# Hybrid encoder step on one core: the order of instructions made with the scheduler's timeline model

## The chip, the cores and the metric

The kernel runs on one core of a Trainium2 chip. TensorE (PE) multiplies matrices and writes its results to PSUM; VectorE (DVE), ScalarE (ACT) and GpSimd (POOL) work on tiles and run beside it; SyncE (SP) mostly issues the transfers. Each engine takes its own instructions in a fixed order, and waits on semaphores for what other engines make. The metric is the device time of one execution in microseconds (us), the median of several.

## The reference

One layer of a streaming encoder for 512 prompt frames and 8 x 16 frames of running streams (640 tokens), model width 2048:

```python
h = rmsnorm(x, p['norm_mix_g'][l])
proj = h @ p['w_in'][l]
...
o_gdn, gdn_conv_new, gdn_S_new = gdn_mixer(...)
...
x = x + jnp.concatenate([o_gdn, o_fox, o_lru], axis=-1) @ p['w_out'][l]
f_out, ffn_conv_new = conv_ffn(rmsnorm(x, p['norm_ffn_g'][l]), ...)
x = x + f_out
```

Three mixers share the input projection: GDN (4 heads, a gated delta rule: per 64-frame chunk a triangular system is solved, then a matrix state is carried on), FoX (8 heads, attention with a forget gate, with a cache of 512 rows for the running streams) and LRU (4 blocks of a gated linear recurrence). The feed-forward part multiplies by `w_up` (two times 5632 columns), convolves and gates, and multiplies by `w_down`. A last norm follows. All of it is fp32.

## The kernel before

Tokens lie along the free dimension, in two halves of 320 columns (`HALF`). Each large matmul is made of three fp32r products, high x high, high x low and low x high: a weight tile is split on ACT into its high part (L134 `whi`, or L1102 `wh` in the feed-forward part) and on DVE into the rest (L135 `wlo`, L1107 `wl`). These 128 x 128 by 320 matmuls (L146 with PSUM tiles `d`, L1143 with PSUM tiles `p`) I call dense.

**Input projection and mixers (to about 860 us).** The heads are projected in the order G0 L0 F0 G1 L1 F1 F2 G2 L2 F3 F4 G3 L3 F5 F6 F7. The mixers are generators that `drive` moves on by one step after each dense piece of work, so that in the source dense matmuls stand between the steps of a mixer. A GDN head solves its triangular system by levels (L628 to L653, a loop over `l` from 1 to 6): PE multiplies M by Z (L633), DVE masks the product (L638), PE multiplies by X (L643), DVE subtracts it from Z (L645), PE transposes Z (L651), ACT copies it back to X (L653). Each step needs the one before. Ahead of the loop stand q and k products (L596), transposes (L517) and copies (L599, L603, L607). The last level takes L618, L621 (ACT), L626 and L628. The PSUM tiles of these steps are `mm` (one buffer) and `m` (three); `d` has three.

**Output projection and norm (to 1223 us).** Two halves, with the first weights of the feed-forward part prepared beside them.

**Up (1223 to 2282 us).** For each of 44 column blocks f, a Winograd-Strassen scheme makes seven products of 8 weight tiles each (`wino`, L1143): seven of the eight PSUM banks are taken by `pf1` in the order of `SEQP`, so that each bank of the next block is one that the block before it used one product earlier. `combine` (L1154 to L1160, with L1435 and L1436 as its gate) reads the seven products and so frees the banks. The weights come by SP; DVE forms three sums of each tile (L1088 to L1090), and L1102 and L1107 split it. `wh` and `wl` have three buffers each, the raw tile `w` five. The gated result goes to HBM (`hT`).

**Down (2282 to 2850 us).** The rows of hT come back as 22 hops of two tiles `f` (L1467, two buffers), whose sums (L1061 to L1063) and split (ACT L1071, DVE L1073) `form` makes, up to 8 hops ahead of the matmuls. 32 visits of `down` make products as above, combine them (L1492 and L1493 in the place of the gate) and add them to HBM. `ending` does the last norm.

**What sets the order.** The source is one program; the tile framework takes all its instructions and orders them on each engine by a model of their times, keeping what depends on what. `drive` and the place in the source only give the priorities. The model is chosen where the context is opened, in the last lines of the program (L1844).

## Time and profile before

| what | us |
|---|---|
| median of 3 runs | 2877.57 (2876.38 to 2877.73) |
| profiled execution | 2873.5 |
| its span, first to last instruction | 2871.7 |
| PE busy | 2827.9 |
| DVE busy | 2141.7 |
| ACT busy | 1034.3 |
| mean granted clock of TensorE | 0.993 |

The profiled execution is 4.1 us below the median. In rows of the profile a line such as L633 is a line of the kernel, followed by the operation, the tile that is written and those that are read, and in square brackets the time that the engine sat idle before it and whose result ended that. Windows give the busy time of each engine between two times, then the granted clock (1.00 is full speed).

### The profile page before, as it was taken

How to read it: one execution, taken by the hardware profiler on the slowest of the kernel's cores; microseconds unless marked ns; L12 is line 12 of the kernel's file. 1: busy time of each engine (PE TensorE's matmuls, PEld its weight loads, DVE VectorE, ACT ScalarE, POOL GpSimd, SP SyncE). 2: the span in 40 equal slices, each digit the busy share in tenths (PEclk: the TensorE clock that was granted, in tenths of full speed). 3: DMA queues.
4: the chain of work that ended last, by engine and by line, in shares of the span. 5: the costliest groups of instructions: out<-in, count | busy, mean ns of one | idle time of the engine just before them, and what ended most of it. 6: DMA issues, size and time to landing. Idle time of an engine off the chain costs nothing. (4 is left out here: it accounts for less than half of the span.)

```text
span 2871.7 us, 51107 instructions
## 1 busy us (share of the span) xinstructions
PE 2827.9 (98%) x19823; PEld 2754.8 (96%) x19823; DVE 2141.7 (75%) x4723; ACT 1034.3 (36%) x1439; POOL 280.5 (10%) x481
## 2 busy tenths in 40 slices
PE   9899999999999999999999999999999999999997
PEld 8899999999999999999999999999999999999997
DVE  5746545644644536898888888988888999898877
ACT  5233323323322413443333333333333444344333
POOL 1000000000000001011101111111111010000003
PEclk9899999999999999999999999999999999999998
DMA  8123143134124646433333333333333365555545
GB/s 302 41 100 113 62 151 124 61 129 140 59 101 166 237 154 197 157 106 102 99 99 97 100 99 104 107 98 100 101 99 99 119 165 160 142 149 150 125 118 140
DMA packets 169060, 356.81 MB, mean 124 GB/s; under 512 B 19432, under 2 KB 24504, under 8 KB 168816
## 3 DMA queue, kind: packets, MB, share of 16 engines
q1 hardware_dynamic: 153104, 306.63, 33.2%
q0 software_dynamic: 15712, 46.91, 7.4%
q8 instruction: 155, 2.54, 0.4%
q14 instruction: 89, 0.73, 0.1%
HBM read 294.07 MB, written 59.39 MB: 123 GB/s over the span
## 5 line engine op out<-in xcount | busy, mean ns | idle before, releaser
L1143 PE MATMUL p<-x,wh 128*128 128x320 f32 x7280 | 1604.8, 309 | 7.2 <-DVE u L1155 2.8
L1143 PEld LDWEIGHTS p<-x,wh 128*128 128x128 f32 x7280 | 1215.9, 188 | 14.9 <-DVE u L1155 4.9
L1143 PE MATMUL p<-x,wl 128*128 128x320 f32 x3640 | 1121.5, 309 | 0.5 <-DVE wl L1107 0.5
L1102 ACT CAST wh<-w 128x896 fp32r<-128x896 f32 x520 | 490.6, 943 | 964.8 <-PE p L1143 705.8
L1143 PEld LDWEIGHTS p<-x,wl 128*128 128x128 f32 x3640 | 682.8, 188 | 0.8 <-DVE wl L1107 0.8
L1107 DVE TENSOR_TENSOR wl<-w,wh 128x896 fp32r<-128x896 f32 x520 | 564.6, 1086 | 116.4 <-ACT wh L1102 74.4
L146 PE MATMUL d<-xh,whi 128*128 128x320 f32 x1488 | 387.8, 326 | 3.1 <-DVE t L218 2.6
L146 PE MATMUL d<-xl,whi 128*128 128x320 f32 x1488 | 365.1, 310 | 0.2 <-DVE xl L184 0.2
L146 PE MATMUL d<-xh,wlo 128*128 128x320 f32 x1488 | 363.0, 310 | 0.2 <-DVE wlo L135 0.2
L134 ACT CAST whi<-raw 128x512 fp32r<-128x512 f32 x226 | 139.4, 619 | 450.1 <-PE d L146 407.4
L135 DVE TENSOR_TENSOR wlo<-raw,whi 128x512 fp32r<-128x512 f32 x226 | 155.1, 688 | 158.3 <-ACT whi L134 157.1
L146 PEld LDWEIGHTS d<-xh,whi 128*128 128x128 f32 x1488 | 250.3, 189 | 12.7 <-DVE t L218 4.1
L146 PEld LDWEIGHTS d<-xl,whi 128*128 128x128 f32 x1488 | 255.6, 188 | 0.8 <-DVE xl L184 0.5
L146 PEld LDWEIGHTS d<-xh,wlo 128*128 128x128 f32 x1488 | 254.6, 188 | 0.7 <-DVE wlo L135 0.4
L1088 DVE TENSOR_TENSOR w<-w 128x256 f32<-128x256 f32 x520 | 216.1, 417 | 51.9 <-DMA w<-in_w_down 48.6
L1090 DVE TENSOR_TENSOR w<-w 128x128 f32<-128x128 f32 x520 | 148.1, 285 | 6.2
L1089 DVE TENSOR_TENSOR w<-w 128x128 f32<-128x128 f32 x520 | 146.7, 284 | 4.1
L257 DVE SCALAR_TENSOR_TENSOR t<-t,prm,t 128x656 f32<-128x656 f32 (+1 forms) x136 | 122.3, 899 | 5.1 <-ACT t L253 4.4
L1429 POOL COPY t<-ns_fc 128x16 f32<-128x16 f32 x44 | 95.6, 2173 | 0.2 <-issue 0.2
L1499 POOL DMA_DIRECT2D x<-t x48 | 42.0, 1018 | 382.9 <-DVE t L1493 358.2
L1073 DVE TENSOR_TENSOR x<-f,x 128x960 fp32r<-128x960 f32 (+1 forms) x58 | 76.2, 1315 | 0.2 <-ACT x L1071 0.2
L1071 ACT CAST x<-f 128x960 fp32r<-128x960 f32 (+1 forms) x58 | 64.1, 1126 | 30.5 <-DVE f L1063 13.5
(420 smaller groups left out, 2851.8 us busy)
## 6 DMA issues: line engine op xcount, KB each, us to landing
w<-in_w_up SPq DMA_DIRECT2D x352, 256.0 KB, 2.6
raw<-in_w_in SPq DMA_DIRECT2D x192, 256.0 KB, 2.7
w<-in_w_down SPq DMA_DIRECT2D x176, 256.0 KB, 2.8
x<-t POOLq DMA_DIRECT2D x80, 320.0 KB, 4.4
kc<-in_ckT SPq DMA_DIRECT2D x32, 512.0 KB, 5.0
vc<-in_cv SPq DMA_DIRECT2D x32, 512.0 KB, 5.6
hT<-t POOLq DMA_DIRECT2D x44, 320.0 KB, 2.5
f<-hT SPq DMA_DIRECT2D x44, 320.0 KB, 3.4
```

The source lines that it names most:

```text
L134: nc.scalar.copy(hi[:, :n], raw[:, :n])
L135: nc.vector.tensor_sub(lo[:, :n], raw[:, :n], hi[:, :n].bitcast(F32))
L146: self.nc.tensor.matmul(ps[h][:, :HALF], wt[:, w], x[:, h * HALF:(h + 1) * HALF], start=start and i == 0, stop=stop and i == 2)
L257: nc.vector.scalar_tensor_tensor(out[:, :n], x[:, j:j + n], w[:, j:j + 1], out[:, :n], op0=OP.mult, op1=OP.add)
L1073: nc.vector.tensor_sub(l3[:, a:b], f[:, a:b], h3[:, a:b].bitcast(F32))
L1088: nc.vector.tensor_tensor(w[:, 4:6], w[:, 0:1].to_broadcast([P, 2, P]), w[:, 2:4], op=OP.add)
L1089: nc.vector.tensor_add(w[:, 6], w[:, 4], w[:, 3])
L1090: nc.vector.tensor_add(w[:, 7], w[:, 1], w[:, 6])
L1102: nc.scalar.copy(hi[:, 0:n], part)
L1107: self.nc.vector.tensor_sub(lo[:, 0:n], part, hi[:, 0:n].bitcast(F32))
L1143: nc.tensor.matmul(ps[p], l[:, wi], r[:, xi], start=i == 0 and j == 0, stop=i == n - 1 and j == 2)
L1429: nc.gpsimd.tensor_copy(so[:, :, :2], ns_fc[:, f, 1:, :])
```

## The change

The scheduler is asked for its other model, which keeps a timeline of the engines; nothing else in the source differs.

```diff
-    with tile.TileContext(nc) as tc:
+    with tile.TileContext(nc, schedule_with_timeline_sim=True) as tc:
         body(tc, a, cfg)
```

The two programs have the same instructions on each engine; their order differs on all of them. Three places follow. Names carry running numbers; `mm`, `m`, `d`, `p` are PSUM tiles, `t` and `u` temporaries.

**PE, first level of the solve of GDN head G1.** Before (from L517, the transposes into mm_448, to the M x Z product, and the first dense matmuls after it):

```order
L517 MATMUL mm_448_2979<-cst0_86,t_441_2936 128x128 x5
L146 MATMUL d_453_3026<-xl0_125,whi_439_2921 128x320
L146 MATMUL d_453_3026<-xh0_123,wlo_440_2922 128x320
L146 MATMUL d_453_3026<-xh0_123,whi_439_2921 128x320
L146 MATMUL d_453_3026<-xl0_125,whi_439_2921 128x320
L146 MATMUL d_453_3026<-xh0_123,wlo_440_2922 128x320
L146 MATMUL d_453_3026<-xh0_123,whi_439_2921 128x320
L633 MATMUL mm_449_2992<-t_442_2937,t_422_2816 128x128 x5
L146 MATMUL d_453_3026<-xl0_125,whi_439_2921 128x320
```

After (dense work, then the same steps from the L517 ahead of them, and on to the X product of the level):

```order
L146 MATMUL d_453_3026<-xl1_126,whi_456_3036 128x320
L146 MATMUL d_453_3026<-xh1_124,wlo_457_3037 128x320
L517 MATMUL mm_444_2959<-cst0_86,t_397_2658 128x128 x5
L517 MATMUL mm_448_2979<-cst0_86,t_441_2936 128x128 x5
L633 MATMUL mm_449_2992<-t_442_2937,t_422_2816 128x128 x5
L643 MATMUL mm_458_3040<-t_450_3004,t_441_2936 128x128 x5
L146 MATMUL d_454_3027<-xh0_123,whi_439_2921 128x320
```

Six dense matmuls stood between the two steps, seven between L633 and L643; now L517, L517, L633 and L643 follow one another directly, and the dense ones stand ahead of them and behind. G2 and G3 have the same rows.

**DVE, where up ends and down begins.** Before (from the low part wl_3473 of one weight tile to that of the next one, wl_3487, and the second half of the same hop):

```order
L1107 TENSOR_TENSOR wl_3473_24706<-w_3449_24562,wh_3472_24705 128x896
L1090 TENSOR_TENSOR w_3452_24592<-w_3452_24592 128x128
L1088 TENSOR_TENSOR w_3466_24664<-w_3466_24664 128x256
L1073 TENSOR_TENSOR x_3489_24787<-f_3474_24730,x_3488_24786 128x960
L1089 TENSOR_TENSOR w_3466_24664<-w_3466_24664 128x128
L1107 TENSOR_TENSOR wl_3487_24762<-w_3452_24592,wh_3486_24761 128x896
L1090 TENSOR_TENSOR w_3466_24664<-w_3466_24664 128x128
L1073 TENSOR_TENSOR x_3489_24787<-f_3474_24730,x_3488_24786 128x1280
```

After (part of what now stands between wl_3473 and wl_3487; `f` are rows of hT, and `x` their split):

```order
L1073 TENSOR_TENSOR x_3583_25353<-f_3568_25296,x_3582_25352 128x1280
L1155 TENSOR_TENSOR u_3477_24738<-p_3460_24658,u_3477_24738 128x320
L1061 TENSOR_TENSOR f_3599_25508<-f_3599_25508 128x640
L1073 TENSOR_TENSOR x_3614_25565<-f_3599_25508,x_3613_25564 128x960
L1156 TENSOR_TENSOR t_3476_24737<-u_3477_24738,p_3461_24659 128x320
L1492 TENSOR_TENSOR t_3475_24736<-u_3477_24738,p_3463_24661 128x320
L1062 TENSOR_TENSOR f_3599_25508<-f_3599_25508 128x320
L1157 TENSOR_TENSOR u_3477_24738<-u_3477_24738,p_3462_24660 128x320
L1158 TENSOR_TENSOR t_3476_24737<-t_3476_24737,p_3462_24660 128x320
L1061 TENSOR_TENSOR f_3630_25720<-f_3630_25720 128x640
L1063 TENSOR_TENSOR f_3599_25508<-f_3599_25508 128x320
L1493 TENSOR_TENSOR t_3475_24736<-p_3465_24663,u_3477_24738 128x320
```

Between those two weight tiles stood four rows; now there are 39, which hold the sums and splits of four later hops (f_3537, f_3568, f_3599, f_3630), a combine of a block and the rest of an up block.

**DVE and PE at a block boundary of up.** DVE before (the combine of one block, and the low part of a weight tile of the next):

```order
L1155 TENSOR_TENSOR t_2331_15536<-p_2300_15289,t_2331_15536 128x320
L1435 TENSOR_TENSOR t_2330_15535<-t_2331_15536,p_2303_15292 128x256
L1156 TENSOR_TENSOR t_2332_15537<-t_2331_15536,p_2301_15290 128x320
L1436 TENSOR_TENSOR t_2330_15535<-t_2331_15536,p_2303_15292 128x4x16
L1157 TENSOR_TENSOR t_2331_15536<-t_2331_15536,p_2302_15291 128x320
L1158 TENSOR_TENSOR t_2332_15537<-t_2332_15537,p_2302_15291 128x320
L1435 TENSOR_TENSOR t_2330_15535<-p_2305_15294,t_2331_15536 128x256
L1160 TENSOR_TENSOR t_2332_15537<-t_2332_15537,p_2304_15293 128x320
L1436 TENSOR_TENSOR t_2330_15535<-p_2305_15294,t_2331_15536 128x4x16
L1107 TENSOR_TENSOR wl_2329_15511<-w_2318_15415,wh_2328_15510 128x896
```

DVE after:

```order
L1155 TENSOR_TENSOR t_2331_15536<-p_2300_15289,t_2331_15536 128x320
L1435 TENSOR_TENSOR t_2330_15535<-t_2331_15536,p_2303_15292 128x256
L1436 TENSOR_TENSOR t_2330_15535<-t_2331_15536,p_2303_15292 128x4x16
L1089 TENSOR_TENSOR w_2327_15505<-w_2327_15505 128x128
L1156 TENSOR_TENSOR t_2332_15537<-t_2331_15536,p_2301_15290 128x320
L1090 TENSOR_TENSOR w_2327_15505<-w_2327_15505 128x128
L1107 TENSOR_TENSOR wl_2329_15511<-w_2318_15415,wh_2328_15510 128x896
L1157 TENSOR_TENSOR t_2331_15536<-t_2331_15536,p_2302_15291 128x320
L1158 TENSOR_TENSOR t_2332_15537<-t_2332_15537,p_2302_15291 128x320
```

The low part wl_2329 and rows of the weight sums have moved in between the rows of the combine. PE before, at the start of the next block (weight tile wh_2322 and its low part, product by product):

```order
L1143 MATMUL p_2333_15563<-x_1801_11575,wh_2322_15450 128x320
L1143 MATMUL p_2333_15563<-x_1802_11576,wh_2322_15450 128x320
L1143 MATMUL p_2333_15563<-x_1801_11575,wl_2323_15451 128x320
L1143 MATMUL p_2334_15564<-x_1801_11575,wh_2322_15450 128x320
L1143 MATMUL p_2334_15564<-x_1802_11576,wh_2322_15450 128x320
L1143 MATMUL p_2334_15564<-x_1801_11575,wl_2323_15451 128x320
L1143 MATMUL p_2335_15565<-x_1801_11575,wh_2322_15450 128x320
L1143 MATMUL p_2335_15565<-x_1802_11576,wh_2322_15450 128x320
```

PE after:

```order
L1143 MATMUL p_2333_15563<-x_1801_11575,wh_2322_15450 128x320
L1143 MATMUL p_2333_15563<-x_1802_11576,wh_2322_15450 128x320
L1143 MATMUL p_2333_15563<-x_1801_11575,wl_2323_15451 128x320
L1143 MATMUL p_2333_15563<-x_1826_11725,wh_2325_15480 128x320
L1143 MATMUL p_2333_15563<-x_1827_11726,wh_2325_15480 128x320
L1143 MATMUL p_2334_15564<-x_1801_11575,wh_2322_15450 128x320
L1143 MATMUL p_2334_15564<-x_1802_11576,wh_2322_15450 128x320
L1143 MATMUL p_2334_15564<-x_1801_11575,wl_2323_15451 128x320
L1143 MATMUL p_2334_15564<-x_1826_11725,wh_2325_15480 128x320
L1143 MATMUL p_2334_15564<-x_1827_11726,wh_2325_15480 128x320
L1143 MATMUL p_2333_15563<-x_1826_11725,wl_2326_15481 128x320
```

Before, a block takes one weight tile through all seven products; now it takes two, and soon three, through a product before the next product begins. The second product's bank, and each later one, is first written later in the block.

## Prediction

> **What bounds the kernel now.** I read the page's busy times first, then the list of what TensorE (PE) waited for, then the timeline around the waits, then windows of the granted clock.
>
> ```profile
> PE 2827.9 (98%) x19823; PEld 2754.8 (96%) x19823; DVE 2141.7 (75%) x4723; ACT 1034.3 (36%) x1439; POOL 280.5 (10%) x481
> ```
>
> PE is busy 2827.9 of 2871.7 us. All idle time of PE together is 43.8 us, so a new order can win at most that; it can lose far more. The matmuls are the same in both orders, so the change is worth the new idle time of PE, less the old, plus what the clock adds.
>
> ```profile
> 98.06 0.31 PE L146 MATMUL d<-xl,whi 128*128 128x320 f32 x1
> ...
> 98.94 0.31 PE L146 MATMUL d<-xl,whi 128*128 128x320 f32 x1
> ```
>
> These are the first and last of seven dense matmuls: six steps in 0.88 us, 0.1467 us each. I call that one matmul of cover: the time it gives a neighbour's answer to come back.
>
> ```profile
> 105.92 1.84 PE L596 MATMUL mm<-t,t 128*128 128x128 f32 x10 [2.92 <-DVE t L585]
> 107.80 0.82 DVE L599 TENSOR_TENSOR t<-mm,t 128x640 f32<-128x640 f32 x1 [0.22 <-PE mm L596]
> ...
> 108.68 1.33 PE L517 MATMUL mm<-cst,t 128*128 128x128 f32 x5 [0.92 <-DVE t L599]
> ...
> 110.92 1.33 PE L517 MATMUL mm<-cst,t 128*128 128x128 f32 x5 [0.92 <-DVE t L603]
> 112.29 0.69 ACT L607 COPY t<-mm 128x640 f32<-128x640 f32 x1 [10.36 <-PE mm L517]
> ...
> 113.03 2.50 PE L633 MATMUL mm<-t,t 128*128 128x128 f32 x10 [0.78 <-ACT t L607]
> 115.57 0.82 DVE L638 TENSOR_TENSOR t<-mm,cst 128x640 f32<-128x640 f32 x1 [4.70 <-PE mm L633]
> ...
> 116.45 1.65 PE L643 MATMUL mm<-t,t 128*128 128x128 f32 x6 [0.92 <-DVE t L638]
> ```
>
> This is the delta-rule chain of the first GDN head, where before has nothing between the steps. Each step of PE needs the answer of the step before from DVE or ACT, and each such round trip leaves PE idle 0.92, 0.92, 0.78 and 0.92 us. In heads G1 to G3 the same rows carry no such wait: there 6 or 7 dense matmuls (0.88 to 1.03 us) stand between the steps and just cover it.
>
> **Half clock.** The windows are 3.41 us; columns are PE, weight loads, DVE, ACT, POOL busy, then the clock.
>
> ```profile
> 89.59:93.00 3.41, 3.41 (x22) 2.78 (x21) 2.41 (x9) 1.01 (x3) 0.00 (x0) 1.00 0.17 61
> 93.00:96.41 3.41, 3.41 (x16) 3.37 (x15) 3.06 (x5) 0.75 (x2) 0.00 (x0) 0.50 0.01 3
> ...
> 113.48:116.90 3.42, 2.50 (x12) 2.21 (x12) 1.33 (x4) 0.00 (x0) 0.00 (x0) 0.50 0.00 0
> 116.90:120.30 3.40, 3.40 (x16) 3.40 (x16) 0.86 (x3) 0.94 (x1) 0.34 (x2) 0.50 0.00 0
> ```
> ```profile
> 1165.00:1170.00 5.00, 3.25 (x17) 3.25 (x17) 5.00 (x8) 2.20 (x3) 0.21 (x1) 0.82 0.39 125
> 1170.00:1175.00 5.00, 5.00 (x31) 5.00 (x31) 3.96 (x8) 0.94 (x2) 0.33 (x1) 0.84 0.66 217
> ...
> 2290.00:2295.00 5.00, 2.57 (x14) 1.71 (x12) 5.00 (x13) 2.00 (x3) 0.68 (x2) 0.96 0.34 134
> 2295.00:2300.00 5.00, 4.58 (x24) 4.58 (x24) 5.00 (x13) 1.26 (x1) 2.22 (x3) 0.70 0.29 79
> ```
>
> After a stretch with little dense work a window of about 3.4 us runs at clock 0.50 and does half its work, so it costs 1.7 us. One follows the stall at 1166 (5 us less 3.25 busy) and one that at 2293; the one at 93 follows a window in which PE was busy throughout, but with tiny matmuls of the GDN chain. So a chain without dense work costs its waits and then a slow window.
>
> [...]
>
> **The change, part by part.** No instruction is added or removed; only places differ. All is against the profiled execution, 2873.5 us (span 2871.7); the median of the three runs is 2877.6, 4.1 higher, and is added at the end.
>
> *First head, 85 to 117 us.* In the new order 51 dense matmuls (7 + 14 + 18 + 6 + 6) no longer stand between the steps L435 to L596 of G0. Bounds: nothing, if the answers come sooner than the cover, and 51 x 0.1467 = 7.5 us. The steps after these, bare in before too, wait each time, so I take **7**. On SP the last tiles of x now stand behind other loads, and the first norm's broadcast (L204) comes 48 dense matmuls later than before; dense work of other columns lies in front of it, so I count nothing.
>
> *Heads G1 to G3, first two levels of the solve.* Now L517, L633 and L643 follow each other with nothing between (the rows are shown in the section on the change). By the four rows above that is 0.92 + 0.78 + 0.92 = 2.6 us, three times: **7.8**.
>
> *All four heads, later levels.* Here 102 matmuls of cover (6 + 8 + 22 + 18 + 18 + 30) go: L651, L633, L204, L643, L651, L618, L626 stand bare, and on DVE two L880 and one L882 come ahead of L638.
>
> ```profile
> L645 DVE TENSOR_TENSOR t<-t,m 128x512 f32<-128x512 f32 x8 | 5.5, 682 | 2.9 <-PE m L643 2.9
> L638 DVE TENSOR_TENSOR t<-m,cst 128x512 f32<-128x512 f32 x8 | 5.4, 681 | 0.0
> ...
> L880 DVE TENSOR_TENSOR t<-t,mm 128x256 f32<-128x256 f32 x8 | 3.0, 417 | 5.9 <-PE mm L204 5.9
> L882 DVE TENSOR_TENSOR t<-t,mm 128x128 f32<-128x128 f32 x4 | 1.1, 280 | 0.0
> ```
> ```profile
> L653 ACT COPY t<-m 128x512 f32<-128x512 f32 x12 | 7.0, 582 | 14.5 <-PE m L651 14.5
> ...
> L621 ACT COPY t<-m 64x256 f32<-64x256 f32 x4 | 1.5, 366 | 10.4 <-PE m L618 10.4
> ```
>
> L643 waits for 2 x 0.42 + 0.28 + 0.68, less the 0.4 that PE spends on the last row ahead: 1.4. L651 waits 0.7 for L645. L626 waits for what is left of L653 + L621 = 0.95 behind L618: 0.6. Sum 2.7, four times: **10.8**.
>
> *Chunk scan of the four heads.* Some 16 steps of the scan and of FoX, 6 dense matmuls apart in before, are now bare, but they come from two independent chains that cover each other. Between nothing and 8 x 0.8 us, I take 1.5; the LRU step L811, which now stands 11 instead of 34 matmuls behind its forerunner, 1. Four times 2.5: **10**.
>
> *Half clock.* Three bare stretches in each of four heads, less G0's first, are 11. At one window of 1.7 us each: **19**. Bounds: nothing, and two windows each, 37.
>
> *FFN up, 1223 to 2282 us.* The DVE rows look alarming: L1107 for the next weights now stands inside the combine that frees the PSUM banks, ahead of L1157 and L1158.
>
> ```profile
> 1517.84 1.09 DVE L1107 TENSOR_TENSOR wl<-w,wh 128x896 fp32r<-128x896 f32 x1 [1.00 <-PE p L1143]
> 1518.85 0.48 DVE L1155 TENSOR_TENSOR t<-p,t 128x320 f32<-128x320 f32 x1
> 1519.25 0.41 DVE L1435 TENSOR_TENSOR t<-t,p 128x256 f32<-128x256 f32 x1
> ```
> ```profile
> 1519.85 0.45 PE L1143 MATMUL p<-x,wh 128*128 128x320 f32 x2
> ```
> ```profile
> 1519.90 0.94 ACT L1102 CAST wh<-w 128x896 fp32r<-128x896 f32 x1 [1.77 <-PE p L1143]
> ```
>
> The next block starts on PE at 1519.85, with the first row shown. That L1107 needs the L1102 at 1519.90, so it starts about 1520.9; one L1107 takes 1.0 us of DVE (1517.84 to 1518.85), then L1157 and L1158 (0.40 from start to start, as L1155 to its neighbour, and 0.48) bring the bank at 1522.8, 2.9 us after 1519.85. In the old matmul order PE would want it at 1519.85 + 12 x 0.1467 = 1521.6, and each of 42 blocks would lose 1.2 us. But the new PE order does two or three weight tiles per product before it goes on, and reaches that bank after 27 matmuls, 3.96 us. So the cost is **0**, with a margin of 1.0 us.
>
> *Start of down, 2282 to 2400 us.* DVE has no room there.
>
> ```profile
> L1073 DVE TENSOR_TENSOR x<-f,x 128x1280 fp32r<-128x1280 f32 x20 | 29.6, 1481 | 0.0
> L1073 DVE TENSOR_TENSOR x<-f,x 128x960 fp32r<-128x960 f32 x19 | 21.8, 1148 | 0.0
> L1061 DVE TENSOR_TENSOR f<-f 128x640 f32<-128x640 f32 x19 | 15.5, 818 | 0.7 <-DMA f<-hT 0.4
> ...
> L1062 DVE TENSOR_TENSOR f<-f 128x320 f32<-128x320 f32 x19 | 9.2, 483 | 0.0
> ```
> ```profile
> 2330.00:2355.00 25.00, 25.00 (x172) 25.00 (x172) 25.00 (x53) 11.43 (x13) 3.49 (x4) 1.00 0.69 164
> ```
>
> Forming one hop of hT costs DVE 1.48 + 1.15 + 0.82 + 2 x 0.48 = 4.4 us, and in this window DVE is busy 25.00 of 25 us. The new order forms five hops more ahead of weight tile wl_3487: 22 us of DVE work that PE's weights now stand behind (39 rows between wl_3473 and wl_3487, four before). PE idles for nearly all of it, since before has no slack here: **20**, between 8 (part of it in gaps of DVE) and 30 (loads of f in the way). Later in down DVE then has less to do, but PE waits for almost nothing there in before, so nothing comes back.
>
> Sum: 2873.5 + 7 + 7.8 + 10.8 + 10 + 19 + 20 = 2948; with the 4.1 to the median **2952 us**.
>
> **Rivals.**
>
> *The clock holds.* Same waits, no slow windows: 2952 - 19 = 2933. For it: the waits are under 1 us each. Against it: the window at 93.
>
> *Up loses after all.* If the margin of 1.0 us is used up (an ACT or DVE row late by more), 42 blocks lose 1.2 us, 50 us: 3002. For it: DVE is nearly full; against: the new matmul order fits.
>
> *Not slower: the answers arrive in time.* Before loses time that a better order wins back:
>
> ```profile
> PE d L146 <- DVE wl L135: 2.5, 1, 2.5
> PE p L1143 <- ACT wh L1102: 2.3, 1, 2.3
> ```
>
> These two, their slow windows (3.4) and small waits in down (about 2) are 10 us, so 2867. It needs the bare chains of G1 to G3 to cost next to nothing: it decides at a round trip of under 0.1 us, where the trace shows 0.78 to 0.92.
>
> *Nothing moves that matters:* within 0.2% (6 us; about what a measurement here tells from no change).
>
> **How the numbers follow.** Forecast 0.60, the clock holds 0.17, up loses 0.12, not slower 0.07, no change 0.04. So faster 0.07, same 0.04, slower 0.89. The low end takes the sum with the lower bounds of the clock and half of the chains, about 2900; the high end takes two slow windows per stretch and 30 us in down, or the up rival: 3005.
>
> **What would show it.** Right: PE waits of 0.7 to 0.9 us on L517, L633, L643 and L651 in all four heads; half-clock windows in the solves of the heads, which before are at 106 to 177, 282 to 352, 514 to 584 and 746 to 816 us; PE waiting for wl L1107 some 20 us in all just after 2300; no waits on L1158 in up. Wrong: up blocks longer than the 168 x 0.1467 = 24.6 us they take now, or heads with PE gapless at bare chains.

## The result, and the profile after

| | before | after |
|---|---|---|
| median of 6 runs each, us | 2877.65 (2875.98 to 2881.85) | 2979.18 (2976.05 to 2984.43) |
| profiled execution, us | 2873.5 | 2980.32 |
| its span, us | 2871.7 | 2978.6 |
| PE idle in the span, us | 43.8 | 110.4 |
| mean granted clock | 0.993 | 0.979 |

The ratio is 1.0352, with a 95% interval of 1.0341 to 1.0363: 101.5 us slower. The forecast was 2952 us, in the range 2900 to 3005.

The page of the kernel after gives the busy times:

```profile
PE 2868.2 (96%) x19823; PEld 2783.1 (93%) x19823; DVE 2148.4 (72%) x4723; ACT 1018.5 (34%) x1439; POOL 223.4 (8%) x481
```

The counts of PE, DVE and ACT are those of before. Of the 106.9 us that the span grew, PE is idle for 66.6 and busy for 40.3. The same matmuls take longer at the lower clock. Before shows it behind the stall at 1166 us: in its window at 0.50 (1168.22 to 1171.63 us) ten dense ones take 2.67 us (1168.40 to 1171.07), 0.267 each, and right behind it, at 1.00, six take 0.88 us (1171.91 to 1172.79), 0.147 each.

```profile
1168.40 0.73 PE L146 MATMUL d<-oh,wh 128*128 128x320 f32 x2
...
1171.07 0.72 PE L146 MATMUL d<-oh,wl 128*128 128x320 f32 x2
...
1171.91 0.46 PE L146 MATMUL d<-ol,wh 128*128 128x320 f32 x2
...
1172.79 0.46 PE L146 MATMUL d<-ol,wh 128*128 128x320 f32 x2
```

The next table cuts both executions at the first and the last L1154 of up and at the first L1524 (where the ending's plain products begin, at 2817.8 us in before; down ends there, not at the 2850 us given with the kernel): windows with their length, then PE, weight loads, DVE, ACT and POOL busy, and the clock. Before:

```profile
0.00:1223.30 1223.30, 1206.26 (x8833) 1142.48 (x8833) 685.70 (x1518) 398.31 (x691) 63.48 (x181) 0.99 0.40 135
1223.30:2282.00 1058.70, 1058.52 (x7217) 1058.38 (x7218) 939.70 (x2116) 408.94 (x480) 137.08 (x219) 1.00 0.33 102
2282.00:2817.80 535.80, 528.11 (x3541) 520.23 (x3540) 477.42 (x996) 210.93 (x244) 56.41 (x66) 1.00 0.57 145
2817.80:2871.70 53.90, 34.98 (x237) 33.73 (x235) 38.86 (x96) 16.12 (x26) 23.52 (x16) 0.84 0.45 132
```

After:

```profile
0.00:1278.60 1278.60, 1225.80 (x8833) 1160.57 (x8833) 686.49 (x1530) 396.99 (x692) 64.74 (x181) 0.97 0.39 129
1278.60:2341.30 1062.70, 1062.38 (x7226) 1062.12 (x7227) 946.67 (x2100) 399.59 (x481) 73.69 (x219) 1.00 0.34 101
2341.30:2916.70 575.40, 541.09 (x3531) 522.73 (x3530) 475.36 (x998) 205.81 (x243) 60.92 (x64) 0.98 0.57 135
2916.70:2978.60 61.90, 38.96 (x237) 37.65 (x235) 39.86 (x97) 16.11 (x27) 24.06 (x17) 0.79 0.38 107
```

Up to the first block of up 55.3 us are lost (35.8 idle, 19.5 busy), in up 4.0, in down 39.6 (26.6 idle, 13.0 busy) and in the ending 8.0. The list of what PE waited for (total, times, longest) names the causes:

```profile
PE p L1143 <- DVE wl L1107: 15.1, 17, 2.6
PE p L1509 <- DVE t L1560: 7.9, 2, 5.2
PE p L1143 <- ACT u L1154: 7.6, 1, 7.6
PE m L643 <- DVE t L638: 6.0, 4, 1.5
...
PE mm L517 <- DVE t L603: 3.7, 4, 0.9
PE mm L643 <- DVE t L638: 3.7, 4, 0.9
PE p L1401 <- DVE r L1412: 3.6, 1, 3.6
PE mm L633 <- ACT t L607: 3.1, 4, 0.8
PE m L651 <- DVE t L645: 3.1, 4, 0.8
```

Waits that come four times are those of the GDN heads, one per head. L1401 stands in the norm ahead of up. In head G1 the timeline of PE has at the first level and at a later one:

```profile
310.37 0.76 PE L517 MATMUL mm<-cst,t 128*128 128x128 f32 x5 [0.92 <-DVE t L603]
311.91 1.38 PE L633 MATMUL mm<-t,t 128*128 128x128 f32 x10 [0.78 <-ACT t L607]
314.21 2.00 PE L643 MATMUL mm<-t,t 128*128 128x128 f32 x9 [0.92 <-DVE t L638]
```
```profile
377.39 1.13 PE L643 MATMUL m<-t,t 128*128 128x128 f32 x8 [1.51 <-DVE t L638]
379.30 1.06 PE L651 MATMUL m<-cst,t 128*128 128x128 f32 x4 [0.78 <-DVE t L645]
381.86 1.11 PE L626 MATMUL m<-t,t 64*64 64x64 f32 x8 [0.46 <-ACT t L621]
```

The start of down, first 89 us, and the rest of it, before and then after:

```profile
2282.00:2370.70 88.70, 84.59 (x556) 82.52 (x555) 87.83 (x185) 38.98 (x46) 12.99 (x16) 0.98 0.65 161
2370.70:2817.80 447.10, 443.51 (x2987) 437.71 (x2986) 389.59 (x812) 171.95 (x198) 43.43 (x50) 1.00 0.56 141
```
```profile
2341.30:2430.00 88.70, 66.97 (x378) 60.18 (x377) 78.18 (x163) 32.13 (x37) 15.42 (x12) 0.87 0.55 139
2430.00:2916.70 486.70, 474.12 (x3155) 462.55 (x3154) 397.18 (x836) 173.68 (x206) 45.50 (x52) 1.00 0.57 134
```

PE idles 21.7 us in the first 89 us (before 4.1), at a clock of 0.87 (0.98), and 12.6 us in the rest (before 3.6).

### The profile page after: what moved, and what is told of

Its sections match the earlier page's. It is cut to its first block, busy times and chain, and to the rows that moved or that the text cites. A ratio compares the mean times of both kernels' runs of the same rounds, so it can differ in the third digit from the quotient of the medians.

```text
span 2978.6 us, 51040 instructions
## 1 busy us (share of the span) xinstructions
PE 2868.2 (96%) x19823; PEld 2783.1 (93%) x19823; DVE 2148.4 (72%) x4723; ACT 1018.5 (34%) x1439; POOL 223.4 (8%) x481
## 4 chain that ended last, share of the span: by engine, by line
PE 84%; DVE 8%; DMA 3%; ACT 2%; issue 2%; POOL 0%; SPq 0%; DVEq 0%; ACTq 0%; POOLq 0%
PE p L1143 46%; PE d L146 26%; PE m L146 3%; DMA w<-in_w_down 3%; DVE wl L1107 2%; PE mm L517 1%; DVE w L1088 1%; PE m L949 1%; DVE x L1073 1%; DVE t L823 1%; PE mm L633 1%; PE m L993 1%; PE mm L925 0%; ACT wh L1102 0%; PE m L986 0%
## 5 line engine op out<-in xcount | busy, mean ns | idle before, releaser
L1143 PE MATMUL p<-x,wh 128*128 128x320 f32 x7280 | 1462.0, 310 | 20.7 <-ACT u L1154 7.6
L1143 PEld LDWEIGHTS p<-x,wh 128*128 128x128 f32 x7280 | 1176.3, 188 | 34.0 <-ACT wh L1102 11.3
L1143 PE MATMUL p<-x,wl 128*128 128x320 f32 x3640 | 954.4, 310 | 15.1 <-DVE wl L1107 15.1
L1143 PEld LDWEIGHTS p<-x,wl 128*128 128x128 f32 x3640 | 640.7, 188 | 20.6 <-DVE wl L1107 20.5
L1107 DVE TENSOR_TENSOR wl<-w,wh 128x896 fp32r<-128x896 f32 x520 | 559.1, 1088 | 120.6 <-ACT wh L1102 63.5
L146 PE MATMUL d<-xh,whi 128*128 128x320 f32 x1488 | 425.1, 317 | 8.5 <-DVE t L218 5.9
L146 PE MATMUL d<-xl,whi 128*128 128x320 f32 x1488 | 420.8, 315 | 0.0
L146 PE MATMUL d<-xh,wlo 128*128 128x320 f32 x1488 | 416.6, 313 | 0.0
L146 PEld LDWEIGHTS d<-xh,whi 128*128 128x128 f32 x1488 | 271.9, 191 | 14.5 <-DVE t L218 6.7
L146 PEld LDWEIGHTS d<-xl,whi 128*128 128x128 f32 x1488 | 271.3, 191 | 0.4 <-issue 0.4
L146 PEld LDWEIGHTS d<-xh,wlo 128*128 128x128 f32 x1488 | 270.6, 190 | 0.8 <-issue 0.5
L253 ACT ACTIVATE t<-t,prm 128x656 f32<-128x656 f32 (+1 forms) x56 | 47.4, 846 | 185.8 <-DVE t L1440 179.8
L146 PE MATMUL d<-oh,whi 128*128 128x320 f32 x272 | 81.2, 311 | 0.4 <-ACT oh L1026 0.4
L146 PE MATMUL d<-ol,whi 128*128 128x320 f32 x272 | 81.0, 310 | 0.1
L146 PE MATMUL d<-oh,wlo 128*128 128x320 f32 x272 | 80.8, 309 | 0.0
```

What stands on the lines that cost most here:

```text
L146: self.nc.tensor.matmul(ps[h][:, :HALF], wt[:, w], x[:, h * HALF:(h + 1) * HALF], start=start and i == 0, stop=stop and i == 2)
L253: nc.scalar.activation(out[:, :n], x[:, :n], AF.Copy, scale=w[:, 0:1])
L1107: self.nc.vector.tensor_sub(lo[:, 0:n], part, hi[:, 0:n].bitcast(F32))
L1143: nc.tensor.matmul(ps[p], l[:, wi], r[:, xi], start=i == 0 and j == 0, stop=i == n - 1 and j == 2)
```

## The experiments

Times are medians; "before" is the kernel before, run beside it on the same chip. The stages are cut as above, from the profiled execution.

| run | us | before | ratio (95%) | to up | up | down | ending |
|---|---|---|---|---|---|---|---|
| before, after (profiles) | | | | 1223 / 1279 | 1059 / 1063 | 536 / 576 | 54 / 62 |
| e1_mix_none | 2873.73 | 2876.95 | 0.9996 (0.9984 to 1.0008) | 1226 | 1059 | 535 | 54 |
| e2_mix_only | 2922.90 | 2876.95 | 1.0160 (1.0130 to 1.0189) | 1272 | 1059 | 537 | 54 |
| e3_tl_pin | 2989.38 | 2876.95 | 1.0391 (1.0361 to 1.0421) | 1290 | 1062 | 574 | 61 |
| e4_tl_form | 2967.24 | 2876.95 | 1.0314 (1.0284 to 1.0344) | 1271 | 1061 | 572 | 63 |
| e5_pe_before | 3032.60 | 2875.04 | 1.0546 (1.0515 to 1.0576) | 1253 | 1117 | 600 | 59 |
| e6_dve_before | 3007.14 | 2875.04 | 1.0457 (1.0427 to 1.0488) | 1309 | 1079 | 562 | 57 |
| e7_pe_dve_before | 2890.07 | 2875.04 | 1.0050 (1.0030 to 1.0070) | 1234 | 1058 | 539 | 56 |
| e8_gaps | 3128.44 | 2875.04 | one execution | 1221 | 1316 | 537 | 54 |
| e9_early_forms | 2899.61 | 2874.65 | 1.0079 (1.0056 to 1.0102) | 1229 | 1078 | 542 | 54 |
| e10_rest_tl | 2926.81 | 2874.65 | 1.0174 (1.0155 to 1.0192) | 1230 | 1063 | 573 | 61 |
| e11_out1_tl | 2873.93 | 2874.65 | 0.9995 (0.9986 to 1.0005) | 1222 | 1059 | 538 | 54 |
| e12_late_tl | 2901.25 | 2875.27 | 1.0091 (1.0070 to 1.0112) | 1229 | 1059 | 550 | 62 |

### Which part of the program loses: e1, e2, e10, e12

A block in the program is ordered by itself, with the model that it names. e1 only closes the block in the kernel before; e2 gives it the timeline model.

```diff
+        with tc.block(name="mix", schedule_with_timeline_sim=True):   # e1: False
             streams = [sg, sf]
             drive(inproj(), streams)
...
             drain(streams)
...
-    with tile.TileContext(nc, schedule_with_timeline_sim=True) as tc:
+    with tile.TileContext(nc) as tc:
```

> The input projection, mixers and first half of the output projection stand in a block of their own, which is scheduled by itself; both parts with the model of before. This is the control for the next run. Expected by every theory: the time of before, within 10 us (a block's edge may cost a few us).

> The same block, scheduled with the timeline model; all behind it with the model of before. Theory (the cost of 102 us lies in separate places: 55 in the mixers by bare chains and the half clock, about 45 in down and the ending): 45 to 60 us over the control, up and down as in before (1059 and 536 us). Rival (the costs are one chain, a delay of the mixers that loads and buffers carry into down): nearly the whole 102 us.

The block costs nothing (2873.73 beside 2876.95). With the timeline model in it, the program loses 46 us to before and 49 to e1, the first stage is 48 us longer than before, and all that follows is as before. So the mixers' loss is made there, and later parts don't depend on it.

e10 is the other half: the kernel after, with every engine in the order of before as far as the mixers reach. A row of instruction numbers is turned into dependences that hold the order and add no wait:

```diff
+        for engine, order in ORDERS.items():    # PE, DVE, ACT, POOL, SP: the order of before
+            pinned(tc, engine, order)
...
+def pinned(tc, engine, packed):
+    traced = {i.name: i for i in list(tc.nc.cur_bb.bb.instructions) if i.engine == engine}
+    before = None
+    for n in np.cumsum(np.frombuffer(zlib.decompress(base64.b85decode(packed)), dtype=np.int32)):
+        i = traced.get(f"I-{n}")
+        if i is None:
+            continue
+        if before is not None:
+            tc.add_manual_dep(i, before.name, mybir.DependencyInfo(mybir.DependencyClass.NoSync, mybir.DependencyReason.DATA), reason="pinned")
+        before = i
```

> The changed kernel, but all engines have the order of before from the start to the end of the first half of the output projection; the timeline model places all behind it. The counterpart to the run of the mixers alone. Theory (the costs lie apart and add up): up begins at 1222 to 1232 us, down and the ending keep their 45 to 50 us more, 2918 to 2932 us. Rival (the delay of the mixers makes part of the cost in down): under 2910 us.

It costs 52 us. 46 + 52 = 98 of the 101.5 us: the two halves add up. Down and the ending are 573 and 61 us, within 3 and 1 us of after, and the waits at the start of down are the same ones (7.6 on ACT's L1154, 2.5 on L1155, 2.0 on the gate).

e12 holds the old order further, through up and the first eight visits of down:

```diff
         for v, end in enumerate(ends):
             drive(down(v % npair, end, g), [[g]])
+            if v == 7:
+                for engine, order in ORDERS.items():
+                    pinned(tc, engine, order)
```

> The timeline model's orders are used only behind the first eight visits of down (about the first 117 us of that part); all ahead of it has the order of before on every engine. Theory, the loss in down is two separate losses: the hops formed ahead of weight tiles at its start (about 29 of the 40 us: 17.6 of waits and 11.5 of half clock in its first 89 us) and small waits later (9 us, and 8 in the ending). Then the start costs nothing here and what is left is 9 + 8, with up to 5 for the seam: 2884 to 2899 us. Rival, the loss lies at the place where the model begins (it orders early what may start early, wherever that is): it then comes back behind the eighth visit in nearly its full size, 2905 to 2925 us. If the later waits were only an after-effect of the start: within 6 us of before.

2901.25 us, 26 more than before and 2 above the upper end. The start of down is as in before (3.8 us idle from 2282 to 2400, before 4.1), and waits come only behind the place where the model's order begins, after 2400 us:

```profile
2340.00:2370.00 30.00, 30.00 (x207) 30.00 (x206) 29.69 (x62) 14.31 (x16) 1.75 (x2) 1.00 0.74 183
...
2400.00:2430.00 30.00, 27.53 (x179) 25.90 (x178) 29.03 (x59) 12.18 (x14) 1.75 (x2) 1.00 0.46 126
```

Down is 14 us longer than before, not 40, and the ending 8. So the rival, a loss that moves to wherever the model begins, doesn't hold at its size (30 to 50 us); the later waits and the ending are no after-effect of the start either. The start is worth about 40 − 14 = 26 us of the loss in down. The remaining 5.7 us stand ahead of up, where all engines have the old order and PE idles no longer (16.6 us up to 1223). The record of the clock has nine windows of 3.41 us at half clock there, and before's has six: three more, at an estimated 1.5 us each (3.41 us of dense matmuls at 0.267 us in place of 0.147), are 4.6 us. These windows lie on a grid of 3.413 us (shown with e8), and one and the same wait of L146 (0.65 us in before, 0.64 in e12) has no slow window behind it in before and one in e12:

```profile
151.05:154.46 3.41, 2.76 (x21) 2.41 (x20) 2.56 (x3) 2.60 (x5) 0.32 (x2) 1.00 0.00 0
154.46:157.87 3.41, 3.41 (x28) 3.39 (x28) 3.23 (x9) 0.13 (x1) 0.00 (x0) 1.00 0.16 43
```
```profile
153.02:156.44 3.42, 2.78 (x22) 2.42 (x21) 2.40 (x5) 2.18 (x4) 0.32 (x2) 1.00 0.00 0
156.44:159.86 3.42, 3.42 (x16) 3.42 (x15) 3.38 (x10) 0.00 (x0) 0.00 (x0) 0.50 0.23 74
```

### One engine's order alone: e3, e5, e6, e7

e3 holds PE alone to the order of the source through the mixers, which keeps dense matmuls between the steps of a head; the other engines are ordered anew by the timeline model.

```diff
+        first_of = len(nc.cur_bb.bb.instructions)
         streams = [sg, sf]
...
         drain(streams)
+        pinned(tc, mybir.EngineType.PE, first_of)   # consecutive PE instructions, as written
```

> The changed kernel, but PE takes its instructions from the start of the input projection to the end of the first half of the output projection in the order of the source, where dense matmuls stand between the steps of a mixer; DVE, ACT and the rest are still placed by the timeline model. Theory (bare chains on PE are the cost in the mixers): 40 to 55 us under the changed kernel, 2925 to 2940 us, with the waits on L517, L633, L643 and L651 in G1 to G3 gone. Rival (the order of DVE and ACT, with weight splits ahead of mixer steps, is the cost): under 15 us won, 2965 us or more.

A miss: 2989.38 us, 10 more than after. The bare first levels are gone (L517 waits 1.3 us for L603 in all, 3.7 in after), but PE now stands in front of other rows. From its list of waits:

```profile
PE mm L811 <- DVE t L645: 17.1, 4, 4.3
...
PE mm L366 <- DVE t L362: 10.1, 1, 10.1
```

L811 is the LRU step: DVE gives the answer it needs behind L645, an instruction of the GDN chain that comes early in DVE's order and late in PE's.

e5 holds PE to exactly the order of before, over the whole program; e6 holds DVE alone; e7 holds both. ACT, POOL and SP keep to the timeline model.

```diff
+        pinned(tc, mybir.EngineType.PE, ORDER_PE)      # e5 and e7
+        pinned(tc, mybir.EngineType.DVE, ORDER_DVE)    # e6 and e7
```

> The changed kernel, but PE has over the whole program exactly the order of before; DVE, ACT, POOL and SP are placed by the timeline model, which still forms eight hops of hT at the start of down. Theory (the place of the matmuls is the cost in the mixers, the early forms on DVE that at the start of down): up begins within 15 us of before, at 1223 to 1238 us; the start of down keeps its 20 us of waits and more; 2905 to 2930 us. Rival (the order of DVE and ACT costs in the mixers): up begins after 1255 us, 2950 us or more.

> The changed kernel, but DVE has exactly the order of before; PE, ACT, POOL and SP are placed by the timeline model. Theory: PE still has most of its bare chains (36 of the steps L517 to L651 follow each other with nothing between; 52 in the changed kernel, 16 in before), so up begins 30 us or more after before's 1223 us; down, without early forms, loses 20 to 30 of its 40 us more; 2930 to 2950 us. Rival (the order of DVE is the whole cost): within 15 us of before.

> PE and DVE have exactly the orders of before, ACT, POOL and SP those that the timeline model finds beside them. Theory (PE and DVE hold the whole cost): within 10 us of before, 2868 to 2888 us. Rival (ACT or the loads on SP hold a share): 2895 us or more.

e5 and e6 missed by some 100 and 60 us: each is slower than after (3032.6 and 3007.1), though each holds one of the two engines to the old order. The model places the other engines anew beside the held one: in e5 only 2214 of DVE's 4723 instructions stand where they stand in after. So these runs compare pairs of orders, and not one engine's order by itself. e7, with both, is at 2890.07, 2 us above what was expected. In e5 the old PE order meets a DVE order in which L1107 stands inside the combine. The waits of e5, then DVE and PE at the start of one block of up:

```profile
PE p L1143 <- DVE t L1158: 31.9, 48, 3.6
PE p L1143 <- DVE t L1493: 20.1, 23, 1.2
PE p L1143 <- DVE t L1436: 11.0, 43, 1.4
```
```profile
1801.98 1.08 DVE L1107 TENSOR_TENSOR wl<-w,wh 128x896 fp32r<-128x896 f32 x1
...
1803.38 0.48 DVE L1158 TENSOR_TENSOR t<-t,p 128x320 f32<-128x320 f32 x1
...
1803.92 0.57 PE L1143 MATMUL p<-x,wh 128*128 128x320 f32 x2 [0.89 <-DVE t L1158]
```

The waits for L1493 all stand in down, 25.6 us of those for L1158 and 9.8 of those for L1436 in up. PE wants the bank (one of the eight PSUM buffers of the kernel's pool `pf`) that L1158 frees and gets it only behind the 1.08 us of L1107. Up is 57.9 us longer than before, 1.3 us for each of 43 blocks. In after, L1107 stands inside the combine too and up has no such wait, since PE's new order asks for that bank later. e6 is the mirror: DVE makes `wl` late for a PE that takes several weight tiles through one product.

```profile
PE p L1143 <- DVE wl L1107: 23.8, 35, 1.4
```

So the loss can't be put down to PE's order or to DVE's alone: it lies in how the two fit, and the pair of before fits better than the pair of after. Of the 15 us that e7 is above before, 11 lie ahead of up; 5.1 of them are one wait of L204 in the first norm, which e10 and e12, with ACT, POOL and SP held as well, don't have.

### The start of down: e4, e9

e4 is the kernel after with the first sum (L1061) and the split (L1073) of each hop kept in program order on DVE, so that a hop can't be formed ahead of the rows that come before it in the source.

```diff
-        nc.vector.tensor_tensor(f[:, 4:6], f[:, 3:4].to_broadcast([P, 2, HALF]), f[:, 1:3], op=OP.subtract)
+        first = nc.vector.tensor_tensor(f[:, 4:6], f[:, 3:4].to_broadcast([P, 2, HALF]), f[:, 1:3], op=OP.subtract)
+        if self.hopping:
+            self.tc.keep_in_program_order(first)
...
+                self.tc.keep_in_program_order(part)    # the L1073 of a hop
```

> The changed kernel, but on DVE the first sum and both splits of each hop of hT come behind the instruction that stands before them in the source, so that the hops are formed one by one during down as in before, not eight at its start. Theory (DVE work that is brought forward starves PE at the start of down): the stretch from 2341 to 2400 us loses its 20 us of waits and its half clock, 25 to 32 us won, 2947 to 2955 us. Rival (the waits come from weight tiles merged three at a time, which have no slack in the three buffers): under 10 us won, with waits on L1107 and L1102 all over down.

Half a miss: 12 us come off, not 25 or more. The idle time in the first 89 us of down falls from 21.7 to 12.5 us and the slow windows there from seven to three, but waits come back later in down, and the stage is only 3 us shorter. The other 8 us come off ahead of up, where PE idles as long as in after (52.6 beside 52.8 us) with 16 slow windows, not 23. This looks like the place of the windows, as in e12, and not like a gain of the hops.

e9 is the reverse, on the kernel before: only the hops are formed early.

```diff
+    def sooner(self):
+        return self.tc.high_priority() if getattr(self, "hopping", False) else ExitStack()
...
+        with self.sooner():     # around L1061 to L1063, L1071, L1073 and the load L1467
```

> The kernel before with one part of the change alone: the loads, sums and splits of the hops of hT have a higher priority, so that DVE forms the first eight hops ahead of the second combine of down (before: two), while PE and all else are placed by the model of before. Theory (early forms starve PE): the start of down waits 15 to 20 us more and falls to half clock, down takes 551 to 566 us (before 536), 2890 to 2907 us in all. Rival (they cost nothing where matmuls keep their order): down within 6 us of 536.

25 us are lost, the size expected, but in another place: in the profiled execution 19 us in the last block of up and 7 in down (5 more stand ahead of up, with nine slow windows and 17.2 us of idle time, before six and 17.0). The first and the last of three windows show DVE full and PE starved:

```profile
2270.00:2290.00 20.00, 11.83 (x64) 11.56 (x64) 19.68 (x29) 10.42 (x11) 0.54 (x1) 0.74 0.42 141
...
2310.00:2330.00 20.00, 13.81 (x57) 12.52 (x58) 20.00 (x45) 6.42 (x8) 3.29 (x4) 0.67 0.37 122
```

Together: early hops alone are enough to lose about 25 us around the seam of up and down, as e12 finds from the other side (26). Holding them back in after gains only 3 us in down; the model places all other rows anew there, and PE waits 9.2 us for the combine's L1155 in place of 1.7. Which rows of that order make the rest of the loss was not tried.

### The clock: e8

e8 adds waits of known length to the kernel before: ahead of 38 blocks of up a chain of ACT copies of growing length, on which a one-column matmul waits. It adds work and leaves nothing out.

```diff
+            nc.scalar.copy(z, self.last)
+            for _ in range(self.gap - 1):
+                nc.scalar.copy(z, z)
+            first = nc.tensor.matmul(ps[1][:, :1], z[:, :P], z[:, :1], start=True, stop=True)
```

> The kernel before with waits put into up: ahead of 38 of its 44 blocks one tiny matmul waits for a chain of 1 to 8 copies on ACT that begins with the last product of the block before, so PE idles about 0.5 to 3.4 us between dense blocks, each length four or five times. It measures from what idle time on a half-clock window follows. Theory (a window of 3.4 us with less than about half of it dense is followed by one at half clock): waits up to 1.2 us never, of 1.5 to 2.2 us sometimes, over 2.4 us nearly always. [...]

Waits of eight lengths came out, from 2.40 to 6.39 us, each four or five times (the very first, of 3.41 us, aside); shorter ones, which I had wanted too, did not. The 2.40 us ones (four) were never followed by a lower clock, the 2.85 us ones (five) each time by one window of 3.41 us at 0.50, and all longer ones, 3.34 to 6.39 us, by slow windows too. First one wait of each; then the two windows of 3.41 us into which the first falls, and of the other the window in which it ends and the one behind that:

```profile
1503.02 0.38 PE L1142 MATMUL p<-gapz 128*128 128x1 f32 x2 [2.40 <-ACT gapz L1139]
1531.00 0.38 PE L1142 MATMUL p<-gapz 128*128 128x1 f32 x2 [2.85 <-ACT gapz L1141]
```
```profile
1498.51:1501.92 3.41, 2.11 (x15) 1.84 (x13) 3.41 (x9) 1.16 (x2) 0.00 (x0) 1.00 0.31 88
1501.92:1505.33 3.41, 2.31 (x16) 2.31 (x17) 3.41 (x10) 1.27 (x2) 0.66 (x2) 1.00 0.22 70
...
1529.23:1532.64 3.41, 1.64 (x11) 1.64 (x12) 3.41 (x9) 1.73 (x3) 0.67 (x2) 1.00 0.18 34
1532.64:1536.05 3.41, 3.41 (x15) 3.41 (x14) 2.59 (x6) 0.23 (x1) 0.00 (x0) 0.50 0.14 51
```

Length alone did not decide: the wait of 2.31 us in before, at 2293 us, had a slow window behind it, those of 2.40 us here had none. The half-clock windows of one execution lie on one grid of 3.413 us (in before and after to 0.01 us): in before three of them start at 93.02, 1168.22 and 2294.62 us, which is 315 and 330 steps of 3.4133 us apart. In up of e8 the idle time of PE within one window of that grid told whether the next was slow: the 2.85 us wait falls on both sides of a grid line as 1.08 + 1.77 us and is followed by a slow window, the 2.40 us one as 1.30 + 1.10 and is not. Over all of up in e8, windows at full clock with 1.51 us of idle time or less were never followed by a slow one, those with 1.9 us or more always were, and between 1.69 and 1.77 us both came (five were, four were not).

### A version to win: e11

Before loses about 2 us at 1166 us, in the output projection; after has no wait there. e11 is the kernel before with the second half of the output projection in the order of after, on PE, DVE, ACT and SP (`pinned` as above, with those rows alone).

> The kernel before, but the second half of the output projection has on PE, DVE, ACT and SP the order of the changed kernel, which has no wait on L135 and no half clock at 1167 us. Theory: 3 to 5 us faster than before, up begins at 1218 to 1220 us, 2871 to 2874 us. Rival (the wait comes from what is behind or ahead of that part): the same time as before within 2 us.

The wait and its slow window are gone, but two other slow windows came in the mixers, so the first stage is only 1 us shorter in the profiled execution, and down is 2 us longer. The ratio of the medians is 0.9995, with at most 4 us to be had by the interval. No order tried here beats before by more than the runs vary.

## Why the prediction was right, and where it was not

The median came out 27 us above the 2952. Against its own execution, 74.6 us were forecast and 106.9 came.

- **Waits of the mixers** (first head 7, first levels 7.8, later levels 10.8, scan 10; 35.6 in all): 35.8 measured up to the start of up, 33.5 of it in the mixers. The first head took 3.7, with 2.6 more ahead of it (the late L204 and what follows it), which were counted at nothing; the scan took what is left, about 8. The other 2.3 lie behind the mixers: PE waits 1.27 and 3.63 us at the norm ahead of up (the longer one is L1401 for L1412, which before doesn't have), and the 2.45 us of before at 1166 are gone. That the totals agree so closely is partly luck. The first levels cost 0.92 + 0.78 + 0.92 in G1, as computed from G0's rows of before. The later ones cost 1.51, 0.78 and 0.46 where 1.4, 0.7 and 0.6 stood. In all, head G1 idles 8.25 us (before 0.63), so 7.6 against 2.6 + 2.7 + 2.5 = 7.8:

```profile
308.00:431.50 123.50, 115.25 (x815) 107.86 (x814) 56.17 (x116) 33.34 (x62) 3.36 (x13) 0.96 0.22 69
```
```profile
282.00:395.00 113.00, 112.37 (x839) 106.74 (x840) 58.01 (x119) 34.12 (x62) 3.36 (x13) 1.00 0.24 78
```

  e2 shows these waits arise in the mixers' order alone. That dense cover makes them vanish was shown only for the pair of orders (e7, e10); cover by PE's order alone brought others (e3).

- **Half clock in the mixers**: 19 forecast, 19.5 us of longer busy time measured up to the start of up, with a different make-up. G1 to G3 have nine slow windows, the count forecast, but 1, 2, 2, 2, 0 and 2 over their stretches ahead of the scan, and one costs less than 1.7 us: PE often idles inside it, and even 3.41 us full of dense matmuls lose only about 1.5 at 0.267 us each in place of 0.147. So such a window does 0.55 of its work (0.147 / 0.267), not half. G0 has more than its two: after 102.9 us the clock stays at 0.50 for 30 us. That stretch of G0:

```profile
102.90:133.00 30.10, 19.79 (x75) 16.23 (x74) 19.62 (x48) 5.32 (x8) 0.93 (x6) 0.50 0.00 1
```

  That the sum fits is partly luck: e4, with the same waits ahead of up, has seven slow windows fewer there and is 8 us shorter. The rival in which the clock holds is out.

- **Up**: 0 forecast, +4.0 with no wait. Of these, about 2.4 (16 dense matmuls at 0.267 us in place of 0.147, and four L1401 that take 0.88 us and not 0.47) are slow windows that begin at 1273.7 us, during the 3.63 us wait in the norm, and last until 1283.9, 5.3 us into up. The argument (PE reaches the bank later than DVE frees it) was right, and the rival's price too: 1.2 us per block forecast for the old matmul order, 1.3 measured in e5.

- **Start of down**: this is the step that failed, by size. 20 us were forecast for all of down, with "nothing comes back" behind the start; 39.6 came. The start itself took about 26 (e12): 17.6 of new idle time and the slower clock, which I had counted in the mixers alone. The kind of wait was half right. `wl` of L1107, forecast at some 20 us, took 7.1 of the 21.2 us of waits in the first 89; the longest is on ACT:

```profile
2363.43 1.26 ACT L1071 CAST x<-f 128x1280 fp32r<-128x1280 f32 x1 [3.69 <-DVE f L1063]
...
2366.53 0.75 ACT L1444 ACTIVATE t<-t 128x656 f32<-128x656 f32 x1 [1.84 <-DVE t L257]
...
2368.33 1.26 ACT L1071 CAST x<-f 128x1280 fp32r<-128x1280 f32 x1 [1.05 <-DVE f L1063]
...
2369.50 0.42 ACT L1154 COPY u<-p 128x320 f32<-128x320 f32 x1
...
2369.97 0.90 PE L1143 MATMUL p<-x,wh 128*128 128x320 f32 x2 [7.56 <-ACT u L1154]
```

  PE waits 7.56 us for a copy of 0.42 us that waits for nothing but its turn: ahead of it in ACT's queue stand the split of two hops and the gate of the last block, each waiting for DVE, and DVE is busy all the time:

```profile
2355.00:2375.00 20.00, 9.30 (x33) 7.83 (x34) 20.00 (x38) 8.11 (x9) 8.38 (x4) 0.52 0.45 150
```

  I had followed the moved hops on DVE alone; each also puts two L1071 into ACT's order. The later part of down, forecast at nothing, has 9 us more idle time (`wl` 7.9 us in ten waits), and e12 shows that it is there without the start.

- **Ending**: not in the sum, +8.0, half of it idle time and half longer busy time at a clock of 0.79 (before 0.84). L1509 waits 7.9 us in two places for L1560 (before 0.7), L1541 3.0 (before 5.1). I had not compared the orders there.

The four terms that were short (down 19.6, ending 8.0, up 4.0, all ahead of up 0.7) are the 32.3 us between 74.6 and 106.9. The low end of the range was not what its terms add up to: without the half clock and half of the waits the sum is 2915 us, not about 2900.

## What to carry to other kernels

The orders of two engines are one plan: holding one of them alone to the old order, with the other placed anew, made this kernel 28 to 53 us slower still; holding both regained nearly all. When an order changes, follow every engine that a moved step issues on, and look at the seams between stages first; a ready copy of 0.42 us that stood in its queue behind starved ones kept PE waiting for 7.56 us. A dependent step of PE without other work beside it cost its round trip here (0.78 to 0.92 us), and the slow windows behind such steps more than half as much again (some 20 us beside 33.5 us of waits in the mixers).

## What the runs showed of the hardware

- Half clock came in windows on a grid of 3.413 us whose place differs between the profiled executions (its first line is 0.86 us into the span in before, 0.52 in after, 0.05 in e8). A dense matmul took 0.267 us in such a window of before and 0.147 us behind it. In up of e8, where the rest of PE's work is dense, the idle time within a grid window told the next: 1.9 us or more was followed by a slow window, 1.51 or less was not, 1.69 to 1.77 both ways. In before, after and e8 a slow window was left after one with at most 0.42 us of idle time (before, from 2294.62), and kept after one with 0.45 (after, from 625.17) or more.
- The number of slow windows differs with the same order: e12, with the order of before ahead of up and as much idle time (16.6 us beside 17.0), has nine there and not six, an estimated 4.6 us at 1.5 us each.
- Waits of 2.31 us (before, 2293) and 2.85 us (e8) had a slow window behind them, one of 2.40 us had not.
- The window from 93.00 in before is at 0.50 after one in which PE counts as busy throughout, with tiny matmuls. In the mixers of after a window with 0.72 us of idle time (from 99.52) was followed by a slow one, and one with 1.70 us (from 799.24) was not. The numbers of e8 don't explain these; they stay open.
